# Three projection columns instead of two computed while the input arrives, in a two-layer attention encoder

## The chip, the cores and the metric

The kernel runs on one core of a Trainium2 chip. The metric is the device time of one execution in microseconds; the kernel before has a median of 868.41 us over 3 runs (867.76 to 868.47). Engine names are those of the profile: PE (TensorE, matrix products), PEld (its weight loads), ACT (ScalarE), DVE (VectorE), POOL (GpSimd), SP (SyncE, which here issues nearly all loads).

## The reference

Two layers over 528 tokens (16 meta tokens and a grid of 8 x 64) with 1024 features:

```python
def hybrid_layer(x, norm_g, w_in, q_norm_g, k_norm_g, rpb, w_o_attn, w_o_na, w_out, cos, sin):
    h = rms_norm(x, norm_g)
    proj = jnp.einsum('bld,de->ble', h, w_in)
    qa, ka, va, za, qb, kb, vb, zb, ga, gb = split_cols(proj)
    qa = apply_axial_rope(rms_norm(qa.reshape(b, l, ATTN_HEADS, HEAD_DIM), q_norm_g), cos, sin)
    ka = apply_axial_rope(rms_norm(ka.reshape(b, l, ATTN_KV_HEADS, HEAD_DIM), k_norm_g), cos, sin)
    oa = gqa_attention(qa, ka, va) * jax.nn.silu(za)
    ob = neighbourhood_attention(qb, kb, vb, rpb) * jax.nn.silu(zb)
    mixed = jax.nn.sigmoid(ga) * (oa @ w_o_attn) + jax.nn.sigmoid(gb) * (ob @ w_o_na)
    return x + mixed @ w_out
```

`gqa_attention` is global attention (8 query heads, 2 key heads, head size 64); `neighbourhood_attention` lets each grid token see a window of the grid and the meta tokens. A last `rms_norm` follows the second layer and the meta tokens are dropped.

## The kernel before, in words

Activations lie transposed: a feature tile is 128 features (partitions) by 528 tokens, and there are 8 feature tiles. Weights come in columns of 128 outputs; `w[l, c]` is column `c` of layer `l`, 128 x 1024. Columns 0 to 3 are the global queries (QA), 4 is KA, 5 is VA; then come QB, KB, VB, ZB, ZA (four each), the gates GA and GB, and the output weights. 

Every operand is split into a high part, rounded to fp32r, and a low part, the rest. A product is then three fp32r products: high x high, low x high and high x low. ACT makes the high part by a copy, POOL (weights) or DVE (activations) the low part by a subtraction. One column for all tokens is 8 feature tiles x 3 products x 2 halves of 264 tokens = 48 products, and each half has a PSUM bank of its own.

The normalisation's factor is not applied to the input of the projection: `normed` (L320) multiplies x by the gain only, into `hh` (ACT, L323) and `hl` (DVE, L324). The sum of squares over the features is made beside it: `squared` on ACT (L330), additions on DVE (L401). `norm_split` splits the sum (`ssh`, `ssl`), `norm_root` turns it into 1/rms (`ms` on PE, `mx` on DVE, a power on POOL), and `norm_spread` lays it out as `rbc`, by which VA and the later columns are multiplied when they are read out of PSUM. The queries and KA are normalised per head instead: `rotated` reads a column out on ACT three times (times the gain, L459; the square, rounded, L460, and not, L461), DVE makes `ql`, PE sums the squares per head (`mh`, L444), and `rotate` applies the rotary tables in four DVE operations (L468 to L471).

At the start `piece` loads the first four row tiles of QA and QA+1 in pairs, 128 KB at a time, `half` their second halves, and `feature` one feature tile of x. The products of QA and QA+1 (L423) run as the tiles arrive; QA+2 and all later columns come through `product` (L309 to L311), for which `weights` loads half columns in the order of the list `order`, three ahead, through buffers `raw` (3), `whi` (4) and `wlo` (4).

A scheduler orders each engine's instructions by their place in the program, by readiness in its own time model and by an urgency mark (`high_priority`); `issue_after` puts an instruction behind a named one on its engine. Side work (norm, heads, attention units) is queued by hand: `product` calls `tick()` after each half of a column, and `side_gqa.later(n, part)` puts a part n ticks later. Attention units start at ticks of a given remainder modulo 4: global units at remainder 0, neighbourhood heads at remainder 1. Columns in the dictionary `first` are read out directly and make no tick. `NORM_AT`, `GQA_AT` and `NA_AT` hold the numbers of ticks. Near the end of layer 0 `side_gqa.finish()` (at the third GA gate) runs what is left; one gate column later the product `y` needs the last head's output.

Of the kernel before, what the change touches and what calls it, by code (L numbers as in the profile page):

```python
# [39 lines left out]
NORM_AT = ({"tokens": (1, 4, 6), "squares": (2, 2, 2, 3, 2), "heads": (2, 3, 5, 7, 6), "values": (1, 4)},  # L40
# [51 lines left out]
def trunk_kernel(ctx: ExitStack, tc: tile.TileContext, xT, w, gn, gf, bias, rope, out):  # L92
# [37 lines left out]
    with tc.high_priority():  # L130
        for _ in range(10):
            nc.tensor.matmul(warm[:, :P], zero, zero, start=True, stop=True)


    gains = cpool.tile([P, DEPTH * KT + KT + 2 * DEPTH], F32, name="gains")
# [61 lines left out]
    for l in range(DEPTH):  # L197
        cols = [QA, QA + 1, QA + 2, QA + 3, KA, VA]
        for j in range(4):
            cols += [KB + j, QB + j, VB + j, ZB + j, ZA + j]  # L200
        order += [(l, c, i) for c in cols for i in range(2)]
        if l == 0:

            order = order[1:2] + order[3:]
        for gate, wo in ((GB, WOB), (GA, WOA)):
            for m in range(8 + LAG):
                order += [(l, gate + m, 0), (l, gate + m, 1)] if m < 8 else []
                order += [(l, wo + (m - LAG) // 2, (m - LAG) % 2)] if m >= LAG else []
        order += [(l, WOUT + m, i) for m in range(8) for i in range(2)] if l < DEPTH - 1 else []
# [110 lines left out]
    def normed(l, k, x, n):  # L320

        hi, lo = slot("h", f"hh{l}_{k}", F32R), slot("h", f"hl{l}_{k}", F32R)
        h_last["hi"] = nc.scalar.mul(hi[:, :n], x, g_in[l][:, k:k + 1])  # L323
        h_last["lo"] = nc.vector.scalar_tensor_tensor(lo[:, :n], x, g_in[l][:, k:k + 1], hi[:, :n].bitcast(F32),  # L324
                                                      op0=ALU.mult, op1=ALU.subtract)
        return hi, lo
# [46 lines left out]
    def piece(c, i):  # L373
        raw = slot("K", f"rawp{c}_{i}")[:, :2 * P]
        hi, lo = (slot("O", f"w{'hl'[v]}p{c}_{i}", F32R)[:, :2 * P] for v in range(2))
        nc.sync.dma_start(raw, w[0, c][:, 2 * P * i:2 * P * (i + 1)])
        done[0] = nc.scalar.copy(hi, raw).ins
        done[1] = nc.gpsimd.tensor_sub(lo, raw, hi.bitcast(F32)).ins
        pieces[c, i] = hi, lo

    def half(c):
        weights(0, c, 1, 1)
        done[:] = split_at["weights"]
# [12 lines left out]
    def input_squares(ks):  # L396
        return [squared(k == 0, xs[k], NTOK, f"0_{k}") for k in ks]

    def sum_up(sqs):
        for sq in sqs:  # L400
            nc.vector.tensor_add(total["ss"], total["ss"], sq)  # L401

    total, late = {}, []
    with tc.issue_after(h_last["hi"].ins), tc.issue_after(h_last["lo"].ins):
        total["ss"], *sqs = input_squares(range(3))
        sum_up(sqs)
    with tc.issue_after(h_last["square"].ins):
        weights(0, QA + 2, 1, 1)
    with tc.issue_after(split_at["weights"][0]):
        sum_up(input_squares((3, 4)))  # L410
        late.append(input_squares((5, 6)))


    first, ends = {}, ((0, HALF), (HALF, NTOK))
    for c, ps in ((QA, [bank(ps_p, f"pp0_{QA}_{a}", "pp")[:, :HALF] for a, _ in ends]),
                  (QA + 1, ps_s.tile([P, 2, 512], F32, tag="S", name=f"pp0_{QA + 1}"))):
        first[c] = [(ps[i] if c == QA else ps[:, i, :HALF], a, b) for i, (a, b) in enumerate(ends)]
    for c, k in sorted(((c, k) for c in first for k in range(KT)), key=lambda x: (x[1] + 2 * (x[0] > QA and x[1] > 3), x[0])):
        wh, wl = (t[:, P * (k % 4):P * (k % 4 + 1)] for t in weights(0, c, k // 4, 1)) if k > 3 else (
            t[:, P * (k % 2):P * (k % 2 + 1)] for t in pieces[c, k // 2])  # L420
        for wt, rt in ((wh, 0), (wh, 1), (wl, 0)):
            for ps, a, b in first[c]:
                nc.tensor.matmul(ps, wt, h[k][rt][:, a:b], start=k == 0 and wt is wh and rt == 0,  # L423
                                 stop=k == KT - 1 and wt is wl)

    for l in range(DEPTH):
# [22 lines left out]
        def rotated(c, g, full, name):  # L449
# [8 lines left out]
            for ps, a, b in project(c, full):  # L458
                nc.scalar.mul(q[:, a:b], ps, g)  # L459
                nc.scalar.activation(qh[:, a:b], ps, AF.Square)  # L460
                evac["last"] = nc.scalar.activation(sq[:, a:b], ps, AF.Square)  # L461
# [99 lines left out]
        for j in range(4):  # L561
# [3 lines left out]
            with tc.issue_after(evac["low"].ins):  # L565
                if l == 0 and j < 2:
                    sum_up(late[j])
                if l == 0 and j == 0:
                    turn = rotate
                    with tc.issue_after(evac["last"].ins):  # L570
                        late.append(input_squares((7,)))
# [616 lines left out]
```

## Time and profile before

| | |
|---|---|
| median of 3 runs | 868.41 us (867.76 to 868.47) |
| profiled execution, its own time | 869.61 us |
| its span, first to last instruction | 867.8 us |
| PE busy | 854.8 us (99%), 5976 products |
| ACT, DVE, POOL busy | 494.2, 537.2, 365.6 us |
| HBM read | 76.72 MB |

The profiled execution is one run with a span from the first to the last instruction; its own time lies 1.2 us above the median. PE is the engine that is busy throughout; the end of a product is modelled, so neighbouring products overlap in the busy time, and the starts are the surer measure.

### The profile page before, as it was taken

How to read it: one execution, taken by the hardware profiler on the slowest of the kernel's cores; microseconds unless marked ns; L12 is line 12 of the kernel's file. 1: busy time of each engine (PE TensorE's matmuls, PEld its weight loads, DVE VectorE, ACT ScalarE, POOL GpSimd, SP SyncE). 2: the span in 40 equal slices, each digit the busy share in tenths (PEclk: the TensorE clock that was granted, in tenths of full speed). 3: DMA queues.
4: the chain of work that ended last, by engine and by line, in shares of the span. 5: the costliest groups of instructions: out<-in, count | busy, mean ns of one | idle time of the engine just before them, and what ended most of it. 6: DMA issues, size and time to landing. Idle time of an engine off the chain costs nothing.

```text
span 867.8 us, 16234 instructions
## 1 busy us (share of the span) xinstructions
PE 854.8 (99%) x5976; PEld 790.6 (91%) x5976; DVE 537.2 (62%) x1277; ACT 494.2 (57%) x1170; POOL 365.6 (42%) x300
## 2 busy tenths in 40 slices
PE   8999999999999999999999999999999999999997
PEld 8999999999999999999998989898988888888786
DVE  5985667676774574436547656677767646454633
ACT  7645677677774555333445456677767645543432
POOL 5564323443223332544764643334333333334751
PEclk9999999999999999999999999999999999999999
DMA  6364253325112222325555664235422222223602
GB/s 223 99 186 145 93 150 99 106 73 153 49 50 75 62 67 81 98 86 152 148 139 127 171 198 130 79 95 151 145 81 73 86 73 73 87 85 97 206 25 97
DMA packets 64671, 95.76 MB, mean 110 GB/s; under 512 B 22864, under 2 KB 23376, under 8 KB 64592
## 3 DMA queue, kind: packets, MB, share of 16 engines
q1 hardware_dynamic: 63872, 93.66, 36.8%
q8 instruction: 47, 0.77, 0.4%
q10 hardware_dynamic: 720, 1.06, 0.3%
q14 instruction: 32, 0.26, 0.1%
HBM read 76.72 MB, written 4.19 MB: 93 GB/s over the span
## 4 chain that ended last, share of the span: by engine, by line
PE 86%; ACT 6%; DVE 4%; DMA 2%; issue 1%; POOL 0%; SPq 0%; POOLq 0%; ACTq 0%; DVEq 0%
PE pp L311 18%; PE pp L309 18%; PE pp L310 17%; PE y L309 4%; PE y L311 4%; PE y L310 3%; PE av L797 3%; PE pt L124 3%; PE avb L940 2%; PE pf L1115 2%; PE S L525 2%; PE pf L1117 2%; PE pf L1116 1%; PE S L526 1%; DMA x<-in_xT_dram 1%
## 5 line engine op out<-in xcount | busy, mean ns | idle before, releaser
L227 POOL TENSOR_TENSOR wlo<-raw,whi 128x512 fp32r<-128x512 f32 x214 | 285.3, 1337 | 425.4 <-ACT whi L226 341.7
L309 PE MATMUL pp<-hh,whi 128*128 128x264 f32 (+1 forms) x1056 | 334.7, 317 | 0.6 <-ACT qs L461 0.5
L311 PE MATMUL pp<-hh,wlo 128*128 128x264 f32 (+1 forms) x1056 | 329.3, 312 | 0.0
L310 PE MATMUL pp<-hl,whi 128*128 128x264 f32 (+1 forms) x1056 | 328.6, 311 | 0.0
L226 ACT CAST whi<-raw 128x512 fp32r<-128x512 f32 x214 | 131.5, 619 | 152.7 <-PE pp L310 58.3
L311 PEld LDWEIGHTS pp<-hh,wlo 128*128 128x128 f32 x1056 | 198.8, 188 | 10.7
L309 PEld LDWEIGHTS pp<-hh,whi 128*128 128x128 f32 x1056 | 198.6, 188 | 10.1 <-ACT qs L461 1.1
L310 PEld LDWEIGHTS pp<-hl,whi 128*128 128x128 f32 x1056 | 199.3, 189 | 9.0
L750 DVE CUSTOM_DVE_ANT_1 P<-S,r 128x528 f32<-128x528 f32 x64 | 45.1, 704 | 18.5 <-PE S L526 17.6
L183 DVE TENSOR_TENSOR ptl<-pt,pth 128x512 fp32r<-128x512 f32 x64 | 44.0, 689 | 18.0 <-ACT pth L182 17.2
L1012 DVE TENSOR_TENSOR mg<-pp,rbc 128x264 f32<-128x264 f32 (+1 forms) x48 | 24.8, 517 | 43.2 <-PE pp L311 42.7
L754 ACT ACTIVATE P<-P,st 128x528 f32<-128x528 f32 x64 | 47.2, 737 | 1.9
L876 ACT ACTIVATE Pb<-Pb,stb 128x208 f32<-128x208 f32 (+1 forms) x64 | 31.1, 487 | 16.6 <-DVE stb L874 16.3
L124 PE MATMUL pt<-ident,P 128*128 128x128 f32 x256 | 39.3, 275 | 0.6 <-DVE ptl L183 0.4
L182 ACT CAST pth<-pt 128x512 fp32r<-128x512 f32 x64 | 37.2, 583 | 4.2 <-PE pt L124 2.9
L1013 ACT ACTIVATE mg<-mg 128x264 f32<-128x264 f32 (+1 forms) x48 | 23.7, 494 | 24.4 <-DVE mg L1012 24.4
L310 PE MATMUL pp<-mx,whi 128*128 128x264 f32 x128 | 36.6, 286 | 0.0
L309 PE MATMUL pp<-mx,whi 128*128 128x264 f32 x128 | 36.4, 285 | 0.0
L311 PE MATMUL pp<-mx,wlo 128*128 128x264 f32 x128 | 36.3, 284 | 0.0
L797 PE MATMUL av<-pth,VA 128*128 128x256 f32 x128 | 35.0, 296 | 0.0
L756 DVE TENSOR_SCALAR P<-P,st 128x528 f32<-128x528 f32 x64 | 33.7, 527 | 2.1
L797 PE MATMUL av<-ptl,VA 128*128 128x256 f32 x128 | 33.1, 281 | 0.0
(526 smaller groups left out, 1764.3 us busy)
## 6 DMA issues: line engine op xcount, KB each, us to landing
raw<-in_w_dram SPq DMA_DIRECT2D x214, 256.0 KB, 2.7
bias<-in_bias_dram SPq DMA_DIRECT2D x16, 480.0 KB, 4.5
KB<-KB SPq DMA_DIRECT2D x24, 280.0 KB, 4.0
rawl<-in_w_dram SPq DMA_DIRECT2D x16, 256.0 KB, 2.9
x<-in_xT_dram SPq DMA_DIRECT2D x8, 264.0 KB, 6.3
xr<-in_xT_dram SPq DMA_DIRECT2D x8, 264.0 KB, 3.9
Q<-q SPq DMA_DIRECT2D x16, 128.0 KB, 2.9
x1d<-xt SPq DMA_DIRECT2D x32, 64.0 KB, 2.8
```

The source lines that it names most:

```text
L124: nc.tensor.transpose(ps, src, ident[:n, :n])
L182: split_at["hi"] = nc.scalar.copy(hi, src)
L183: split_at["any"] = nc.vector.tensor_sub(lo, src, hi.bitcast(F32))
L226: cast = nc.scalar.copy(hi, raw)
L227: sub = nc.gpsimd.tensor_sub(lo, raw, hi.bitcast(F32))
L309: nc.tensor.matmul(ps, wh, rh[:, a:b], start=i == 0, stop=False)
L310: nc.tensor.matmul(ps, wh, rl[:, a:b], start=False, stop=False)
L311: nc.tensor.matmul(ps, wl, rh[:, a:b], start=False, stop=i == n - 1)
L750: newest["max"] = nc.vector.tensor_tensor_reduce(p[:n].rearrange("p (i k) -> p i k", i=2), S[:n, :, :HALF], scale[:n].unsqueeze(2).to_broa ...
L754: nc.scalar.activation(p[:n], p[:n], AF.Exp, bias=st[:n, 1:2], scale=1.0, accum_out=st[:n, 2:3])
L756: nc.vector.tensor_scalar_mul(p[:n], p[:n], st[:n, 3:4])
L797: nc.tensor.matmul(c["av"], rows2(c["t"][i][0]), c["t"][i][1], start=i == 0, stop=i == 8)
```

## The change

- QA, QA+1 and QA+2 run with the input. Their weights are laid out on the host by row tiles: `w3[k]` holds the 128 inputs of feature tile k for all 384 outputs, 192 KB in one piece. `row_tile(k)` loads and splits it in front of `feature(k)`; the loads of weights and x are put in turn on SP. `w3[0]` is loaded from ACT's queue, ahead of the gains.
- hh of feature tile 0 is made in two halves of the tokens.
- Squares are computed and added along with the tiles, three tiles behind; tiles 6 and 7 are added after QA and QA+1 are read out. The first half column of QA+3 is cast after the sixth square.
- The products go tile by tile over three columns up to tile 3, and then in a written order. QA+2 gets two PSUM banks of another pool (`avn`, `avg`).
- The read-outs in `rotated` follow each other on ACT. In layer 0 the ticks of `norm_split`, `norm_root`, `norm_spread` are 1, 2, 4 instead of 1, 4, 6, those of the first two sums of squares per head 1, 1 instead of 2, 2, and `meta_columns` 4 instead of 5. QA+2 makes no ticks any more.
- 7 warming products instead of 10 (two records each).

```diff
-NORM_AT = ({"tokens": (1, 4, 6), "squares": (2, 2, 2, 3, 2), "heads": (2, 3, 5, 7, 6), "values": (1, 4)},
+NORM_AT = ({"tokens": (1, 2, 4), "squares": (1, 1, 2, 3, 2), "heads": (2, 3, 5, 7, 6), "values": (1, 4)},
...
-        for _ in range(10):
+        for _ in range(7):
             nc.tensor.matmul(warm[:, :P], zero, zero, start=True, stop=True)
+    w3 = w[0, QA:QA + 3].rearrange("c p n -> (c p n)").rearrange("(k p n) -> k p n", k=KT, p=P)
+    raw3 = {0: slot("K", "rawp0")[:, :3 * P]}
+    nc.scalar.dma_start(raw3[0], w3[0])
...
-            order = order[1:2] + order[3:]
+            order = order[6:]
...
-    def normed(l, k, x, n):
+    def normed(l, k, x, n, spans=None):
         hi, lo = slot("h", f"hh{l}_{k}", F32R), slot("h", f"hl{l}_{k}", F32R)
-        h_last["hi"] = nc.scalar.mul(hi[:, :n], x, g_in[l][:, k:k + 1])
+        for a, b in spans or ((0, n),):
+            h_last["hi"] = nc.scalar.mul(hi[:, a:b], x[:, a:b], g_in[l][:, k:k + 1])
...
-    def piece(c, i):
-        raw = slot("K", f"rawp{c}_{i}")[:, :2 * P]
-        hi, lo = (slot("O", f"w{'hl'[v]}p{c}_{i}", F32R)[:, :2 * P] for v in range(2))
-        nc.sync.dma_start(raw, w[0, c][:, 2 * P * i:2 * P * (i + 1)])
...
+    def row_tile(k):
+        if k not in raw3:
+            raw3[k] = slot("K" if k < 4 else "E", f"rawp{k}")[:, :3 * P]
+            in_turn(raw3[k], w3[k])
+        hi, lo = (slot("O", f"w{'hl'[v]}p{k}", F32R)[:, :3 * P] for v in range(2))
+        done[0] = nc.scalar.copy(hi, raw3[k]).ins
+        done[1] = nc.gpsimd.tensor_sub(lo, raw3[k], hi.bitcast(F32)).ins
+        pieces[k] = hi, lo
     def feature(k):
         if k % 2 == 0:
             xs.extend(two("M", f"x0_{k}"))
-        nc.sync.dma_start(xs[k], xT[k])
-        h.append(normed(0, k, xs[k], NTOK))
+        in_turn(xs[k], xT[k])
+        h.append(normed(0, k, xs[k], NTOK, ((0, HALF), (HALF, NTOK)) if k == 0 else None))
         done[0] = h_last["hi"].ins
-    for part in ((piece, QA, 0), (feature, 0), (piece, QA + 1, 0), (feature, 1), (piece, QA, 1), (piece, QA + 1, 1),
-                 (feature, 2), (feature, 3), (half, QA), (feature, 4), (half, QA + 1), (feature, 5), (feature, 6), (feature, 7)):
-        in_order(lambda: part[0](*part[1:]))
...
+    for k in range(KT):
+        in_order(lambda: row_tile(k))
+        in_order(lambda: feature(k))
+        if k > 2:
+            in_order(lambda: add_up(k - 3))
+    in_order(lambda: add_up(5))
+    in_order(next_weights)
...
+    def first_products(c, k):
+        wh, wl = (t[:, P * (c - QA):P * (c - QA + 1)] for t in pieces[k])
+        for wt, rt in ((wh, 0), (wl, 0), (wh, 1)):
+            for ps, a, b in first[c]:
+                nc.tensor.matmul(ps, wt, h[k][rt][:, a:b], start=k == 0 and wt is wh and rt == 0,
+                                 stop=k == KT - 1 and rt == 1)
+    for k in range(4):
+        for c in range(QA, QA + 3):
+            first_products(c, k)
+    for c, k in ((0, 4), (1, 4), (0, 5), (1, 5), (0, 6), (2, 4), (0, 7), (1, 6), (1, 7), (2, 5), (2, 6), (2, 7)):
+        first_products(QA + c, k)
...
             for ps, a, b in project(c, full):
-                nc.scalar.mul(q[:, a:b], ps, g)
-                nc.scalar.activation(qh[:, a:b], ps, AF.Square)
-                evac["last"] = nc.scalar.activation(sq[:, a:b], ps, AF.Square)
+                with ExitStack() as held:
+                    if "last" in evac:
+                        held.enter_context(tc.issue_after(evac["last"].ins))
+                    nc.scalar.mul(q[:, a:b], ps, g)
+                    nc.scalar.activation(qh[:, a:b], ps, AF.Square)
+                    evac["last"] = nc.scalar.activation(sq[:, a:b], ps, AF.Square)
...
                 if l == 0 and j < 2:
-                    sum_up(late[j])
+                    with tc.issue_after(evac["last"].ins):
+                        add_up(6 + j)
...
-                    side_gqa.later(5, meta_columns)
+                    side_gqa.later(4, meta_columns)
...
+    w[0, QA:QA + 3] = w_in[0][:, :3 * P].reshape(3, P, KT * P)
```

More of the change, by code (lines that the diff above doesn't have):

```diff
@@ L371, in in_order @@
             part()
-    def piece(c, i):
-        raw = slot("K", f"rawp{c}_{i}")[:, :2 * P]
-        hi, lo = (slot("O", f"w{'hl'[v]}p{c}_{i}", F32R)[:, :2 * P] for v in range(2))
-        nc.sync.dma_start(raw, w[0, c][:, 2 * P * i:2 * P * (i + 1)])
[L377 to L383, printed above, removed]
+    def row_tile(k):
[6 more added lines that the diff above has]
+        pieces[k] = hi, lo
     def feature(k):
@@ L396, in input_squares @@
[L396 to L411, printed above, removed]
+    total = {}
@@ new lines, in square, with add_up, next_weights @@
+    def square(k):
+        sq = squared(k == 0, xs[k], NTOK, f"0_{k}")
+        done[0] = h_last["square"].ins
+        return sq
+    def add_up(k):
+        sq = square(k)
+        if k == 0:
+            total["ss"] = sq
+        else:
+            nc.vector.tensor_add(total["ss"], total["ss"], sq)
+    def next_weights():
+        weights(0, QA + 3, 0, 1)
+        done[:] = split_at["weights"]
+    for k in range(KT):
[3 more added lines that the diff above has]
+            in_order(lambda: add_up(k - 3))
@@ L414, in trunk_kernel @@
+    in_order(lambda: add_up(5))
+    in_order(next_weights)
     first, ends = {}, ((0, HALF), (HALF, NTOK))
+    two_banks = ps_s.tile([P, 2, 512], F32, tag="S", name=f"pp0_{QA + 1}")
     for c, ps in ((QA, [bank(ps_p, f"pp0_{QA}_{a}", "pp")[:, :HALF] for a, _ in ends]),
[L416 to L421, printed above, removed]
+                  (QA + 1, [two_banks[:, i, :HALF] for i in range(2)]),
+                  (QA + 2, [bank(ps_a, f"pp0_{QA + 2}_{tag}", tag)[:, :HALF] for tag in ("avn", "avg")])):
+        first[c] = [(ps[i], a, b) for i, (a, b) in enumerate(ends)]
```

3 lines of the change are left out of this document (removed).

## The prediction

> **What bounds the kernel now.** I read the page first, then the granted clock and busy time in chosen stretches, then the start in order of time, engine by engine, and last the waits of PE.
>
> ```profile
> span 867.8 us, 16234 instructions
> PE 854.8 (99%) x5976; PEld 790.6 (91%) x5976; DVE 537.2 (62%) x1277; ACT 494.2 (57%) x1170; POOL 365.6 (42%) x300
> 5.33:26.74 21.41, 19.63 (x146) 18.25 (x146) 15.69 (x22) 18.37 (x39) 10.87 (x9) 1.00 0.57 193
> PE pp L423 <- DVE hl L324: 1.3, 3, 0.7
> PE pp L309 <- ACT qs L461: 0.5, 1, 0.5
> PE S L526 <- DVE KA0l L516: 0.5, 1, 0.5
> ```
>
> PE is busy nearly all the span, and the number of products does not change, so only PE's pauses can be won. Busy time hides short ones, because the modelled ends overlap. I count starts instead, in the timeline of PE:
>
> ```profile
> 1.04 4.64 PE L132 MATMUL warm<-zero 128*128 128x128 f32 x20 [1.04 <-DVE one L138]
> 5.33 0.76 PE L423 MATMUL pp<-hh,whp 128*128 128x264 f32 x2
> 5.91 0.42 PE L423 MATMUL pp<-hl,whp 128*128 128x264 f32 x2
> 16.04 0.40 PE L423 MATMUL pp<-hl,whi 128*128 128x264 f32 x2
> 19.94 0.40 PE L423 MATMUL pp<-hh,wlo 128*128 128x264 f32 x2
> 20.79 0.39 PE L309 MATMUL pp<-hh,whi 128*128 128x264 f32 x1 [0.46 <-ACT qs L461]
> 26.74 0.28 PE L444 MATMUL mh<-qh,means_r 128*10 128x264 f32 x1
> ```
>
> From 16.04 to 19.94, 32 products start without a break: 3.90 / 32 = 0.122 us each. A unit, one weight column of one feature tile, is 6 products, 0.731 us. The first three q columns are 24 units, 17.55 us, and end where the row `mh` starts, at 26.74, having begun at 5.33. So 21.41 - 17.55 = 3.9 us of that stretch are pauses. That, and a little before 5.33, is all the change can win at the start.
>
> The pauses come from ACT and DVE, which make the operands as the input lands:
>
> ```profile
> 4.07 0.73 ACT L323 ACTIVATE hh<-x,gains 128x528 fp32r<-128x528 f32 x1 [0.75 <-DMA x<-in_xT_dram]
> 7.05 0.70 ACT L377 CAST whp<-rawp 128x256 fp32r<-128x256 f32 x2
> 10.18 0.74 ACT L323 ACTIVATE hh<-x,gains 128x528 fp32r<-128x528 f32 x1 [1.26 <-DMA x<-in_xT_dram]
> 12.89 2.16 ACT L323 ACTIVATE hh<-x,gains 128x528 fp32r<-128x528 f32 x3
> 16.56 1.13 ACT L226 CAST whi<-raw 128x512 fp32r<-128x512 f32 x2
> 17.59 2.24 ACT L330 ACTIVATE sq<-x 128x528 f32<-128x528 f32 x4
> 6.40 6.47 DMA x<-in_xT_dram
> ```
>
> The last row is of the chain of waits: x7 lands at 12.87. Two columns are 1.46 us of PE work for each feature tile, while the first four tiles come (10.18 - 4.07) / 3 = 2.0 us apart.
>
> **The change part by part.**
>
> *Three columns per feature tile (gain, 3.1 us).* With three units (2.19 us) a tile, PE should fall behind the input and stop waiting. The first product starts when the first half of hh0 is done: x0 moves to the front of SP's queue, but 192 KB of weights travel beside it instead of 128 KB, so I leave hh0 at 4.1; half of it takes about 0.4. PE then does four products, waiting for wlp0 and hl0, until about 5.5, and the first unit ends near 5.95. The other 23 units take 16.8, to 22.8.
>
> From the fourth feature tile on the suppliers are as tight as PE. ACT does per tile a cast of 384 columns (between 0.35 each in the row with 256 and 0.56 in the one with 512: 0.46), hh (2.16 / 3 = 0.72) and a square (2.24 / 4 = 0.56): 1.74 us. DVE does hl and an addition of squares, and these depend on what POOL does beside them:
>
> ```profile
> 4.84 0.77 DVE L324 SCALAR_TENSOR_TENSOR hl<-x,gains,hh 128x528 fp32r<-128x528 f32 x1 [2.54 <-ACT hh L323]
> 16.43 1.50 DVE L401 TENSOR_TENSOR sq<-sq,sq 128x528 f32<-128x528 f32 x2
> 18.26 3.10 DVE L401 TENSOR_TENSOR sq<-sq,sq 128x528 f32<-128x528 f32 x2 [0.32 <-ACT sq L330]
> 7.51 1.74 POOL L378 TENSOR_TENSOR wlp<-rawp,whp 128x256 fp32r<-128x256 f32 x2 [1.30 <-ACT whp L377]
> 17.24 3.56 POOL L227 TENSOR_TENSOR wlo<-raw,whi 128x512 fp32r<-128x512 f32 x2 [2.66 <-ACT whi L226]
> ```
>
> An addition takes 0.75 before POOL's 17.24 and 1.55 beside it. POOL will subtract for eight row tiles of 384 columns, some 1.1 us each (0.87 for 256, 1.78 for 512), so about 60% of DVE's time has POOL beside it: 0.9 + 1.2 = 2.1 us a tile against PE's 2.19. With 1.55 for every addition, hl5, hl6 and hl7 come late by some 1.7 in all and the three columns end at 24.5; with 0.75 for each, at 22.8. I take 23.6, nearer the 60%. 26.74 - 23.6 = 3.1 us (2.2 to 3.9).
>
> [...]
>
> *The loads.* In front of x7 go 8 x 192 = 1536 KB of weights instead of 1024 KB. The window before it moved about 395 KB/us at the end:
>
> ```profile
> GB/s 0 0 0 0 0 95 236 266 214 338 370 278 308 289 222 273 111 175 309 287 292 284 348 366 308 255 301 354 384 408 409 368 416 410 389 407 405 409 396 393
> ```
>
> 512 / 395 = 1.3 us, so x7 lands at 14.2, while PE reaches (0,7) after some 18.5. Four microseconds cover it; without them it would be 1.3 us. On SP the loads stand in turn, w1 behind x0; w0 leaves ACT's queue ahead of `gains`, which may hold hh0 by a few tenths (inside the 0.8 between the bounds). Casts of row tiles 4 to 7 need the O buffers of tiles 0 to 3, which PE releases from 7.4 on, before ACT gets there.
>
> *Fewer warming products (nothing, to 1.5 us lost).* 14 instead of 20 records, 4.64 / 20 = 0.23 each, end at about 4.2 instead of 5.5. PE was slow until about 5.9: the pair at 5.33 took 0.76, the next one 0.42. The gap until the first real product is a tenth or two, so I take nothing.
>
> *The weights of the fourth column (loss, 0.5 us).* Only the first half of QA+3 is cast ahead. The second is wanted 12 products after 23.6, at 25.1. In the old order ACT cast the later weights only between evacuations:
>
> ```profile
> 19.74 0.46 ACT L459 ACTIVATE q<-pp,gains 128x264 f32<-128x264 f32 x1
> 24.39 1.65 ACT L226 CAST whi<-raw 128x512 fp32r<-128x512 f32 x3
> 25.08 4.48 POOL L227 TENSOR_TENSOR wlo<-raw,whi 128x512 fp32r<-128x512 f32 x3 [4.28 <-ACT whi L226]
> ```
>
> If it stays there, at 24.4, POOL's part (4.48 / 3 = 1.5) is done at 26.6 and PE waits 1.5; if ACT takes it in the pause before QA is finished, nothing. Evacuations of the three columns in a row are the worst case, 2 us. I take 0.5. The bank wait of 0.5 in the row of waits lies inside the stretch counted above and goes with it: QA is read out while the other columns run.
>
> *The order written for the sums (loss, 0.5 us).* A column in `first` makes no tick, so QA+2 no longer makes two. `norm_split` stays one tick after QA, but that tick is now in QA+3, and `norm_root` follows one tick later, not three. What it waits for:
>
> ```profile
> 27.59 0.64 ACT L182 CAST ssh<-sq 128x528 fp32r<-128x528 f32 x1
> 30.05 1.79 DVE L469 TENSOR_TENSOR qr<-qr,sin 128x528 f32<-128x528 f32 x1
> 31.76 0.69 DVE L183 TENSOR_TENSOR ssl<-sq,ssh 128x528 fp32r<-128x528 f32 x1
> 33.57 0.16 PE L356 MATMUL ms<-means_r,ssh 128*128 128x2 f32 x1
> ```
>
> Now ssl ends 1.1 before PE asks. After, PE asks at 23.6 + 0.5 + 2 x 2.93 + 1.0 (eight mh products) = 31.0; ssh again follows the mh products, which free its buffers, at about 27.8, and ssl two DVE operations of up to 1.8 later: 29.8 to 32.4. PE waits nothing to 1.4; half a microsecond is taken. Behind ms stands all of KA.
>
> *Attention later by two ticks (gain, 0.5 us).* The first global unit starts at the tick divisible by four that it had, 12, now after VB0 and not after QB0. The wait for KA0l (0.5 in the row) is covered by a product more. At the layer's end the last unit finishes inside the cover of one gate:
>
> ```profile
> 347.94 0.28 PE L797 MATMUL av<-pth,VA 128*128 128x256 f32 x1
> 351.32 0.71 DVE L183 TENSOR_TENSOR oa_3b<-oa,oa_3a 128x528 fp32r<-128x528 f32 x1 [0.70 <-ACT oa_3a L182]
> 354.39 0.28 PE L309 MATMUL y<-oa_0a,whi 128*128 128x264 f32 x1
> ```
>
> oa_3 is ready 2.4 us before y starts. After, transposes and their split (about 1.3 for ACT and DVE), meta and sums fall behind that gate too, some 2.4 more, so the cover is just used up: 0 to 1.5, taken at 0.2.
>
> Sum: 3.1 - 0.5 - 0.5 + 0.5 - 0.2 = 2.4 us. The profiled execution would go from 867.8 to 865.4 in span, and from 869.61 to 867.2 in its own time, which is 1.2 above the median shown; the median goes from 868.41 to 866.0.
>
> **The rivals.** *DVE sets the pace further on.* It runs without pause until 57:
>
> ```profile
> 21.70:57.00 35.30, 35.20 (x290) 33.97 (x289) 34.48 (x62) 19.98 (x48) 20.52 (x17) 1.00 0.50 141
> 45.11 0.28 PE L444 MATMUL mh<-ql,means_r 128*10 128x264 f32 x1
> 48.26 0.42 DVE L664 TENSOR_TENSOR va<-pp,rbc 128x264 f32<-128x264 f32 x1
> 48.74 0.39 PE L309 MATMUL pp<-hh,whi 128*128 128x264 f32 x1
> ```
>
> The first half of VA was finished before 44.8 and was read at 48.26; its bank was taken again at 48.74. If DVE keeps its order and moves only by the one addition it has already done, 0.7, PE waits for that bank and the time is 867.7. Against it: the evacuation is marked urgent, so an earlier PE puts it ahead of rotations, which the later first unit lets wait.
>
> *The root comes too early (slower).* If the third column's split and rotation (0.7 + 0.8 + 1.8 + 1.8 + 0.7 = 5.8 beside POOL) stand in front of ssl on DVE, it ends at about 37, PE stands 6 us before ms, and the time is 868.4 - 2.9 + 6 = 871.5. It decides from the point where ssl ends later than 31.0 + 2.9 = 33.9; over 0.2% it needs 35.6. For it: the split now lies one column later in program order. Against: it is marked urgent, and in the rows above it came between the products of a rotation.
>
> *The clock opens later.* The granted clock of the quoted stretch is 1.00, but PE was slow from 1.04 to 5.9, 4.9 us. If the pause after the shorter warming made that time start over at 4.2, half rate would last to 9.1, and 3.2 us of it cost 1.6: 867.6. Against it: the pause is short beside 4.9. [...]
>
> **How the numbers follow.** A measurement of this kernel tells 0.2%, 1.7 us, from no change. The forecast, a gain of 1.8 or more, holds 0.55 (its own range 864.3 to 866.6); DVE's pace 0.22 and the clock 0.08, both within 0.2%; the early root 0.15, of which 0.12 over 0.2% slower. So faster 0.55, same 0.33, slower 0.12. The range goes from 864.3, all terms at their good ends, to 869.6, which takes in the rivals of no change and some of the early root.
>
> **What would show it.** Three columns ending on PE before 24.5, with waits of PE for hl under 1.7 us in all; x7 landed before 15; a cast of QA+3's second half before 24.5; no wait of PE at ms; S of the first unit without a wait, after VB0; from 60 us on PE's rows as before but 2 to 3 us earlier. It is wrong if PE waits at ms, at `pp` for `va`, or at y in the layer's tail by more than 1.5, or if a slow pitch lasts beyond 7 us.

## The result: 0.5% slower, and where the time went

| | before | after |
|---|---|---|
| median of 6 runs each, one chip | 868.53 us (867.76 to 869.32) | 873.57 us (871.28 to 874.54) |
| ratio, 95% interval | | 1.0052 [1.0038, 1.0066] |
| profiled execution, own time; span | 869.61; 867.8 us | 873.49; 871.7 us |

The prediction said 866.0 us (864.3 to 869.6). The profiled execution after lies at its median; the one before lies 1.1 us above its own. I therefore profiled the kernel before a second time (e11: own time 868.77, span 867.0) and compare with that. Its gain on the first lies at the start, as its first three columns end at 25.60 and not at 26.74, and 0.8 us of it is still there at layer 1. The page of after begins:

```profile
span 871.7 us, 16225 instructions
PE 855.4 (98%) x5970; PEld 792.1 (91%) x5970; DVE 532.9 (61%) x1277; ACT 493.7 (57%) x1171; POOL 366.9 (42%) x300
```

The work is the same, so the starts tell more. I cut each execution at three products: the first one, the first one after the three columns, the first `rk` (the factors of KA, before the first attention unit), and the first `mh` of layer 1. Rows are stretch, length, busy time by engine (PE, PEld, DVE, ACT, POOL), granted clock, DMA share and GB/s. The second profile of before, then after:

```profile
5.32:25.60 20.28, 19.08 (x147) 18.22 (x147) 14.92 (x22) 18.32 (x39) 10.55 (x9) 1.00 0.58 202
25.60:57.46 31.86, 31.80 (x263) 30.58 (x260) 29.79 (x54) 16.46 (x37) 20.49 (x17) 1.00 0.53 149
57.46:458.69 401.23, 398.78 (x3225) 389.87 (x3223) 245.25 (x625) 229.56 (x565) 163.37 (x130) 1.00 0.36 103
```

```profile
5.89:25.27 19.38, 19.38 (x145) 19.24 (x146) 16.12 (x15) 16.32 (x35) 14.73 (x13) 0.91 0.66 223
25.27:60.23 34.96, 33.56 (x262) 32.06 (x261) 27.96 (x60) 18.64 (x44) 18.24 (x15) 0.95 0.45 121
60.23:463.50 403.27, 398.99 (x3224) 390.18 (x3223) 242.72 (x625) 229.10 (x564) 163.58 (x130) 1.00 0.36 102
```

The three columns end at 25.27 instead of 25.60: 0.3 us won, where 3.1 was forecast. The way to `rk` then takes 34.96 instead of 31.86 us, 3.1 lost. The 400 us from there to layer 1, where the diff touches nothing, take 403.27 instead of 401.23, 2.0 lost; the remainder is the same within 0.1. The sum, 4.7, is the difference of the two executions' times (873.49 - 868.77).

*At the start* PE waits for its first operand, then runs at half rate:

```profile
1.04 3.29 PE L132 MATMUL warm<-zero 128*128 128x128 f32 x14 [1.04 <-DVE one L142]
5.89 0.51 PE L432 MATMUL pp<-hh,whp 128*128 128x264 f32 x2 [1.56 <-ACT hh L328]
9.11 0.64 PE L432 MATMUL pp<-hh,whp 128*128 128x264 f32 x2
12.14 0.40 PE L432 MATMUL pp<-hh,whp 128*128 128x264 f32 x2
```

ACT, which makes that operand, and the loads from ACT's queue (count, size, us from issue to landing):

```profile
4.64 0.51 ACT L383 CAST whp<-rawp 128x384 fp32r<-128x384 f32 x1 [1.50 <-DMA rawp<-in_w_dram]
5.32 0.92 ACT L328 ACTIVATE hh<-x,gains 128x264 fp32r<-128x264 f32 x2 [0.17 <-DMA gains<-in_gains_dram]
```

```profile
rawp<-in_w_dram ACTq DMA_DIRECT2D x1, 192.0 KB, 3.9
gains<-in_gains_dram ACTq DMA_DIRECT2D x1, 14.0 KB, 4.1
```

The first weights are there at 4.6 and the gains at 5.3, and `hh` of tile 0, which the prediction put at 4.1, begins at 5.32. The products at 9.11 take 0.64 a pair, those at 12.14 0.40. The two stretches in which the clock was half:

```profile
7.54:10.96 3.42, 3.42 (x18) 3.42 (x17) 3.42 (x3) 3.42 (x8) 3.42 (x4) 0.50 1.04 360
38.26:41.68 3.42, 3.42 (x18) 3.42 (x17) 3.42 (x7) 1.11 (x4) 2.11 (x4) 0.50 0.54 144
```

By these rows, 3.42 us at a granted clock of 0.50 cost 1.7. One of them lies in each of the first two stretches; neither is in the second profile of before. (Before the first opening the granted clock stands at 1.00 even where products are slow, in e1's profile from 4.2 to 10.2, and the mean clock of a run leaves it out: 0.999 in the profile of e7, which opened at 9.6. So a late opening is read from the pace of the products: a pair of 128x264 takes 0.64 at half rate and 0.40 at full.)

*Behind the three columns* PE stands at `ms`. Rows of the list of PE's waits over the whole execution (total, times, longest):

```profile
PE vtd L693 <- DVE na L747: 2.0, 6, 0.7
...
PE Sm L543 <- DVE st L767: 1.5, 1, 1.5
...
PE ms L361 <- DVE ssl L187: 0.8, 1, 0.8
PE mh L459 <- DVE ql L481: 0.6, 1, 0.6
PE pt L124 <- DVE VB L187: 0.6, 1, 0.6
...
PE pp L313 <- DVE mg L1029: 0.4, 1, 0.4
```

The wait for KA0l, 0.5 before, is gone, as the prediction said. In its place `vtd` has 2.0 instead of 1.3, and Sm (1.5), VB (0.6) and mg (0.4) are new, all in the attention. Between 58 and 463 us, where the second profile of before has these two as its longest,

```profile
PE pt L124 <- DVE P L756: 0.6, 1, 0.6
PE S L526 <- DVE KA0l L516: 0.5, 1, 0.5
```

all waits of PE add up to 2.2 us there and to 4.2 in after: the difference is the 2.0 lost. The largest, on PE and then on DVE and POOL at that place:

```profile
264.44 0.34 PE L543 MATMUL Sm<-KA0h,Q2m 128*64 128x264 f32 x1 [1.50 <-DVE st L767]
...
261.84 1.80 DVE L736 TENSOR_TENSOR ob<-ob,zb 128x528 f32<-128x528 f32 x1
263.67 0.71 DVE L767 CUSTOM_DVE_ANT_1 P<-S,r 128x528 f32<-128x528 f32 x1
261.79 2.98 POOL L231 TENSOR_TENSOR wlo<-raw,whi 128x512 fp32r<-128x512 f32 x2 [1.67 <-ACT whi L230]
```

The scores S of a global unit are ready when DVE has just begun the last product of a neighbourhood head (`ob` by its gate). That product takes 1.80 us beside POOL's subtraction, the softmax's maximum waits for it, and the next scores, Sm, wait for the softmax to free their bank.

### The profile page after: what moved, and what is told of

Same layout as the page of the kernel before. It is cut to its first block, busy times and chain, and to the rows that moved or that the text cites. A ratio compares the mean times of both kernels' runs of the same rounds, so it can differ in the third digit from the quotient of the medians.

```text
span 871.7 us, 16225 instructions
## 1 busy us (share of the span) xinstructions
PE 855.4 (98%) x5970; PEld 792.1 (91%) x5970; DVE 532.9 (61%) x1277; ACT 493.7 (57%) x1171; POOL 366.9 (42%) x300
## 3 DMA queue, kind: packets, MB, share of 16 engines
q1 hardware_dynamic: 63728, 93.46, 37.1%
## 4 chain that ended last, share of the span: by engine, by line
PE 88%; ACT 5%; DVE 4%; issue 1%; DMA 1%; POOL 0%; POOLq 0%; ACTq 0%
PE pp L315 18%; PE pp L313 18%; PE pp L314 18%; PE y L313 4%; PE y L315 4%; PE y L314 3%; PE av L814 3%; PE pt L124 3%; PE avb L957 2%; PE pf L1132 2%; PE S L543 2%; PE pf L1134 2%; PE pf L1133 1%; PE S L544 1%; PE pp L432 1%
## 5 line engine op out<-in xcount | busy, mean ns | idle before, releaser
L231 POOL TENSOR_TENSOR wlo<-raw,whi 128x512 fp32r<-128x512 f32 x210 | 279.8, 1336 | 425.7 <-ACT whi L230 326.5
L313 PE MATMUL pp<-hh,whi 128*128 128x264 f32 (+1 forms) x1040 | 330.2, 318 | 0.4 <-DVE mg L1029 0.4
L315 PE MATMUL pp<-hh,wlo 128*128 128x264 f32 (+1 forms) x1040 | 325.7, 313 | 0.0
L314 PE MATMUL pp<-hl,whi 128*128 128x264 f32 (+1 forms) x1040 | 324.7, 312 | 0.0
L230 ACT CAST whi<-raw 128x512 fp32r<-128x512 f32 x210 | 129.0, 619 | 156.0 <-PE pp L314 61.0
L315 PEld LDWEIGHTS pp<-hh,wlo 128*128 128x128 f32 x1040 | 196.4, 189 | 10.7
L313 PEld LDWEIGHTS pp<-hh,whi 128*128 128x128 f32 x1040 | 196.3, 189 | 9.7 <-DVE mg L1029 0.6
L314 PEld LDWEIGHTS pp<-hl,whi 128*128 128x128 f32 x1040 | 196.9, 189 | 8.9
L771 ACT ACTIVATE P<-P,st 128x528 f32<-128x528 f32 x64 | 47.2, 738 | 1.9
L814 PE MATMUL av<-pth,VA 128*128 128x256 f32 x128 | 35.2, 296 | 0.0
```

The lines of the kernel that those rows point to most:

```text
L230: cast = nc.scalar.copy(hi, raw)
L231: sub = nc.gpsimd.tensor_sub(lo, raw, hi.bitcast(F32))
L313: nc.tensor.matmul(ps, wh, rh[:, a:b], start=i == 0, stop=False)
L314: nc.tensor.matmul(ps, wh, rl[:, a:b], start=False, stop=False)
L315: nc.tensor.matmul(ps, wl, rh[:, a:b], start=False, stop=i == n - 1)
L771: nc.scalar.activation(p[:n], p[:n], AF.Exp, bias=st[:n, 1:2], scale=1.0, accum_out=st[:n, 2:3])
```

## The experiments

The main theory is that of the phase: the shift of the attention by one product puts neighbourhood heads and global units into each other's way. Its rivals: the loss is at the start, by late operands or by the clock; the order written for the sums (`ms` too early) costs it; and, from the prediction, DVE's pace takes back what the start wins. Where an expectation names a theory by a letter, C is the phase. Ratios are to the kernel before, run on the same chip.

**Three warming products more (e1).**

```diff
-        for _ in range(7):
+        for _ in range(10):
```

> The changed kernel with 10 warming products again (20 records, to about 5.3 us). Theory A, the granted clock: the pause of PE from 4.2 to 5.9 us is what put the clock to half from 7.5 to 11.0; without the pause the clock stays open there, the three columns end near 23.6 instead of 25.3, and the execution is 1 to 1.7 us shorter than the changed kernel's 873.5, near 872. The second slow window, after the pause at ms, stays. Rival B, the input alone: the start at 5.9 is set by the landing of the first weights, the warming only fills the pause; then the columns end at 25.3 as before and the time is that of the changed kernel within 0.5.

Measured: 872.65 us (870.93 to 873.89), 1.0040 [1.0026, 1.0053], against after's 1.0052: the intervals overlap. In its profile the clock opened only at 10.2, although PE had been warming to 5.68, and it closed again later:

```profile
37.52:40.94 3.42, 3.42 (x17) 3.42 (x17) 3.42 (x6) 0.58 (x2) 3.19 (x5) 0.50 0.44 110
```

Ten products did not open the clock earlier here (10.2) than seven in after (4.1), and the three stretches together lose as much as in after. The number of warming products is not the main cause.

**The first weights by SP's queue (e2).**

```diff
-    nc.scalar.dma_start(raw3[0], w3[0])
+    nc.sync.dma_start(raw3[0], w3[0])
```

> The changed kernel with the first row tile of weights issued by SP, ahead of x0, and only the gains from ACT's queue. Theory A: the late start comes from the first weights and the gains sharing the DMA engines with later tiles from the other queue; on SP in turn they land by 3.3 and 3.1, hh0 starts by 4.4, PE's first product by 4.9, the pause behind the warming is under 0.8 us, the clock stays open, and the three columns end near 23. Gain over the changed kernel 1.5 to 2.5 us, to 871 to 872. Rival: first tiles land late because eight transfers share the engines whichever queue issues them; hh0 starts at 5.0 or later and the time moves by under 0.5.

Measured: 871.50 us (870.53 to 872.65), 1.0036 [1.0023, 1.0048]. ACT has its operands 1.3 to 1.5 us earlier:

```profile
3.18 0.51 ACT L383 CAST whp<-rawp 128x384 fp32r<-128x384 f32 x1 [0.52 <-DMA rawp<-in_w_dram]
4.07 0.92 ACT L328 ACTIVATE hh<-x,gains 128x264 fp32r<-128x264 f32 x2 [0.38 <-DMA x<-in_xT_dram]
```

The first product starts at 4.64 instead of 5.89. The three stretches:

```profile
4.64:24.28 19.64, 18.69 (x144) 17.92 (x145) 16.35 (x15) 16.48 (x35) 14.10 (x13) 1.00 0.70 248
24.28:57.76 33.48, 32.10 (x263) 30.60 (x262) 30.78 (x61) 18.75 (x44) 18.18 (x15) 1.00 0.47 125
57.76:461.25 403.49, 399.03 (x3224) 390.21 (x3223) 243.27 (x625) 228.99 (x564) 164.27 (x130) 1.00 0.36 102
```

The granted clock is 1.00 from start to `rk` here, so these rows show the change without a half-rate stretch: the columns end 1.3 earlier than before (24.28 against 25.60), `rk` comes 0.3 later than before, and the attention still loses 2.3 (403.49 against 401.23). The late start is not enough to explain the loss.

**The root later (e3).** The third sum of squares per head comes one tick later too.

```diff
-NORM_AT = ({"tokens": (1, 2, 4), "squares": (1, 1, 2, 3, 2), ...
+NORM_AT = ({"tokens": (1, 3, 4), "squares": (1, 1, 3, 3, 2), ...
```

> The changed kernel with norm_root one tick later (tokens 1, 3, 4) and the third sum of squares per head one tick later (squares 1, 1, 3). Theory A: PE's waits for ql (0.9) and ssl (1.0) at 32 to 36 us go, and with them the slow window from 38.3 to 41.7; VA begins 1.5 to 3 us earlier and the execution gains as much, to 870.5 to 872. Rival: DVE is the pace there, and PE waits the same time at the read-out of VA or at KB0; then VA's or KB0's products start no earlier, and the time stays within 0.5 of 873.5.

Measured: 871.95 us (870.66 to 872.07), 1.0038 [1.0026, 1.0051]. The wait at `ms` is gone, and so is the second half-rate stretch; a wait of 0.5 at `rb` for POOL's root takes its place. `rk` comes at 58.7 instead of 60.2, about the 1.7 that such a stretch costs. All five runs have a mean granted clock of 0.998; the two runs of after whose clock closed least (0.999) took 871.6 on average, no more. So what e3 wins by its median looks like the clock's, and the attention still takes 403.2 us (58.68 to 461.90).

**The two ticks of QA+2 given back (e4).**

```diff
                     evac["last"] = nc.scalar.activation(sq[:, a:b], ps, AF.Square)
+                if l == 0 and c == QA + 2:
+                    tick()
...
-NORM_AT = ({"tokens": (1, 2, 4), "squares": (1, 1, 2, 3, 2), ...
+NORM_AT = ({"tokens": (1, 4, 6), "squares": (2, 2, 2, 3, 2), ...
...
-                    side_gqa.later(4, meta_columns)
+                    side_gqa.later(5, meta_columns)
```

> The changed kernel with two ticks made at the read-out of QA+2, one for each half, and the numbers of ticks of the kernel before, so that norm, heads and attention units stand beside the same products as before. Theory C: the shift by two ticks is what costs PE 2.3 us between 60 and 400 us (waits at Sm 1.7, at vtd and mg 1.2, at pt 0.7) and the waits at ms and mh 1.9 with the clock's second window 1.7; with the ticks back, the second layer starts within 0.5 of the kernel before, and the time is 868 to 870. Rival: DVE is behind from the start, so the waits move to KA0l at the first global unit (more than 2 us) and the time stays above 871.

Measured: 871.90 us (871.72 to 872.44), 1.0042 [1.0029, 1.0054], not the 868 to 870 expected. Two effects of opposite sign. The old tick numbers put `rb` ahead of its root, one wait:

```profile
PE rb L567 <- POOL rx L197: 3.0, 1, 3.0
```

That and another half-rate stretch (37.1 to 40.5; the run's mean clock is 0.996, e3's 0.998) bring `rk` to 61.63. But from there to layer 1 it takes 400.17 us:

```profile
61.63:461.80 400.17, 398.70 (x3225) 389.98 (x3224) 244.80 (x625) 229.63 (x564) 163.16 (x130) 1.00 0.37 103
```

So the ticks act on the attention as the theory of the phase says; the start and the order for the sums are not mended by them.

**Only the attention's phases (e5).** Without touching the start, the remainders at which units begin move by two ticks:

```diff
-GQA_AT_TICK, NA_AT_TICK = (0, 0), (1, 1)
+GQA_AT_TICK, NA_AT_TICK = (2, 2), (3, 3)
```

> The changed kernel with the remainders at which attention units start moved by two (global units 2 for 0, neighbourhood heads 3 for 1, both layers), so that the units stand beside the products as in the kernel before, while the norm stays as changed. Theory C, the units' place: from the products rk of layer 0 to the first mh of layer 1 the changed kernel lost 2.4 us against the kernel before (offsets 1.6 and 4.0); with the units back it loses nothing there or wins up to 0.7, and the time falls by 2 to 3, to 870 to 871.5; the long gap of 1.8 before Sm is gone. Rival: that loss comes from the time that the start lost, as units and read-outs collide in any place; then the offset still grows by more than 1.5 us.

Measured: 869.03 us (867.46 to 870.46), 1.0009 [1.0000, 1.0018]. Against after the median is 4.5 us lower; by the ratios, which allow for the chip, 3.7. The second and third stretch, and DVE at the place of the long wait:

```profile
25.11:60.07 34.96, 33.55 (x263) 32.06 (x262) 28.01 (x60) 18.63 (x44) 18.23 (x16) 0.95 0.44 120
60.07:460.41 400.34, 398.79 (x3224) 390.05 (x3223) 244.82 (x625) 229.65 (x564) 162.99 (x130) 1.00 0.36 103
```

```profile
258.90 0.71 DVE L736 TENSOR_TENSOR ob<-ob,zb 128x528 f32<-128x528 f32 x1
```

Everything up to `rk` is as in after, 34.96 us, with its `ms` pause and half rate. The attention takes 400.34 instead of 403.27, 2.9 less; the waits at Sm, VB and mg are absent, and the gate's product takes 0.71, with POOL idle beside it. All waits of PE between 58 and 463 us add up to 1.3 instead of 4.2, which is the same 2.9. The rest of the difference goes with how often the clock closed in the runs: those of e5 with a mean clock of 0.998 or 0.999 average 868.5, those of after with 0.999 871.6, again 3 apart. e5 moves the remainders in layer 1 too, where no tick had been taken away; from its first `mh` to the end the kernel takes 408.3 us, as before (408.3) and after (408.2). The phase is shown as the larger part of the loss.

**The converse: the kernel before, with the ticks shifted (e8).** QA+2 makes no ticks, and `NORM_AT` and `meta_columns` get after's numbers:

```diff
-NORM_AT = ({"tokens": (1, 4, 6), "squares": (2, 2, 2, 3, 2), ...
+NORM_AT = ({"tokens": (1, 2, 4), "squares": (1, 1, 2, 3, 2), ...
...
-            tick()
+            if (l, c) != (0, QA + 2):
+                tick()
```

> The kernel before, with two columns at the start, but QA+2 makes no ticks and the norm has the changed numbers of ticks (1, 2, 4; 1, 1, 2). Theory C: the shift of the attention units and of the norm alone costs what the changed kernel shows, 2 to 4 us without any change of the start; from rk to layer 1 it loses 2 to 2.5. Rival: the shift is harmless with the old start; the time stays within 0.7 of 868.5.

Measured: 876.51 us (876.42 to 876.82), 1.0095 [1.0081, 1.0108]. With the old start the attention loses the same:

```profile
63.42:466.55 403.13, 398.82 (x3224) 389.98 (x3223) 242.93 (x625) 228.94 (x564) 163.91 (x130) 1.00 0.36 102
```

Its longest waits of PE:

```profile
PE ms L357 <- DVE ssl L183: 2.3, 1, 2.3
...
PE Sm L526 <- DVE st L751: 1.5, 1, 1.5
```

The wait at Sm is there again with the same 1.5. The shorter delay of the root costs 2.3 at `ms` here and two half-rate stretches in a row (35.1 to 41.9), so that `rk` comes at 63.4; that part depends on the start, and it makes the whole loss 8.4 us, more than the 2 to 4 expected.

**Fewer warming products in the kernel before (e7).**

```diff
-        for _ in range(10):
+        for _ in range(7):
```

> The kernel before with 7 warming products instead of 10, nothing else. The pause of PE lasts from 4.2 to about 5.0 us (hh0 is ready at 4.8). Theory A, the granted clock: in the executions in which a slow window falls on 7 to 11 us the start loses up to 1.7 us; over several executions the median is 0.3 to 1.5 us longer and the times scatter more. Rival: a pause of under 1 us does not matter to the clock, and the start may even come earlier by 0.3; the time stays within 0.3 of the kernel before.

Measured: 868.44 us (867.81 to 870.04), 1.0005 [0.9997, 1.0014]. In its profile the clock opened at 9.6 and the three columns ended at 25.9, 0.3 later than in the second profile of before. The warming is worth 0.05%, not told from nothing.

**All mends together (e6).** The edits of e1, e2, e3 and e5 in the kernel after:

```diff
+        for _ in range(10):
+    nc.sync.dma_start(raw3[0], w3[0])
+NORM_AT = ({"tokens": (1, 3, 4), "squares": (1, 1, 3, 3, 2), ...
+GQA_AT_TICK, NA_AT_TICK = (2, 2), (3, 3)
```

> The changed kernel with four repairs: first weights by SP, 10 warming products, the root one tick later (tokens 1, 3, 4, squares 1, 1, 3), and the units' remainders moved by two. If the costs found so far stand side by side, the three columns end near 24.3 (as with the first weights by SP), the waits at ms and the second slow window are gone, and the middle of layer 0 loses nothing: 866.5 to 868.5. If DVE sets the pace between 25 and 60 us, the early end of the three columns is lost again at rb, at the read-out of VA or at KA0l, and the time is 868.5 to 870.

Measured: 868.01 us (867.32 to 869.47), 0.9999 [0.9990, 1.0008]: its median is 5.6 us below after's, and it is no better than before. The medians of the four alone lie 0.9 + 2.1 + 1.6 + 4.5 = 9.1 below after's, so the gains don't add up; in part the mends take away the same half-rate stretches. The three stretches:

```profile
5.32:23.71 18.39, 17.93 (x146) 17.73 (x146) 16.41 (x15) 16.12 (x34) 13.62 (x10) 1.00 0.72 252
23.71:56.86 33.15, 32.00 (x263) 30.52 (x262) 30.79 (x61) 18.71 (x44) 19.05 (x15) 1.00 0.44 126
56.86:457.33 400.47, 398.66 (x3224) 390.04 (x3223) 245.30 (x625) 229.53 (x564) 163.55 (x130) 1.00 0.36 103
```

Now the three columns end at 23.7, the 23.6 of the prediction, 1.9 earlier than before. Of that 1.3 is given back by `rk`. (This execution is the quickest of the eleven of e6, 0.7 below their median, and the second profile of before lies 0.3 above its own; so about 1 us by which e6 is ahead in these rows is the choice of executions.) DVE is the engine to look at. From the first product to `rk` it is busy 14.92 + 29.79 = 44.7 us before and 16.41 + 30.79 = 47.2 here, for the same 74 instructions: the eight `hl` take 10.0 us instead of 6.8 and the seven additions of squares 7.7 instead of 6.3, and the other work takes 2 less. In the second stretch DVE is busy 93% of the time in both. ACT is busy as long as before (34.8).

**Eight warming products for ten, in e6 (e9).**

```diff
-        for _ in range(10):
+        for _ in range(8):
```

> The four repairs of e6 with 8 warming products instead of 10, so that the warming ends at 4.4 and does not hold the first product (hh0 is ready at 4.5). If the start is still what counts, the three columns end 0.5 to 0.7 earlier than in e6 and the time is 867.3 to 867.7. If DVE sets the pace up to 60 us, the time stays at 868.0 within 0.3, whatever the start wins.

Measured: 868.17 us (867.41 to 868.85), 0.9996 [0.9988, 1.0005]. The first product comes 0.7 earlier (4.64), the columns end at 23.75 and `rk` comes at 56.9, as in e6. An earlier first product alone gives nothing. That the suppliers then set the end of the columns is an inference: PE's only wait there is again 0.5 for `hl`.

**Stacked pairs one column later (e10).** This kernel has e9's eight warming products, though its expectation calls it e6.

```diff
-            if j > 1:
-                stack_pair(j - 2)
+            if j > 1 + (l == 0):
+                stack_pair(j - 2 - (l == 0))
...
+        if l == 0:
+            stack_pair(1)
```

> e6 with the stacking of the query pairs one column later in layer 0, so that ACT's copy of Q no longer stands, waiting 1.9 us for the rotation, in front of the read-out of QA+3 and of ssh. Theory D, the order on ACT: KA's first bank comes free and ssh is made about 2 us earlier, PE's waits at mh (0.9) and rb (0.8) go, and the time falls by 1 to 1.7, to 866.3 to 867. Rival, DVE or its buffers: the read-out waits for a buffer that a rotation frees, the gaps stay or move to KA0l at the first global unit (now 0.8), and the time stays within 0.4 of 868.

Measured: 867.93 us (867.07 to 869.12), 0.9994 [0.9985, 1.0003]; e9, from which it is one edit away, has 868.17. The wait at `rb` is gone, and a longer one at the third sum of squares stands in its place. The row of PE's waits, and the timeline with DVE's rotation ahead of `ql`, a later one, POOL, and the two halves of the sum of squares:

```profile
PE mh L459 <- DVE ql L481: 1.8, 1, 1.8
```

```profile
30.43 1.79 DVE L487 TENSOR_TENSOR qr<-qr,sin 128x528 f32<-128x528 f32 x1
32.14 0.69 DVE L481 TENSOR_TENSOR ql<-qs,qh 128x528 fp32r<-128x528 f32 x1
35.71 0.70 DVE L487 TENSOR_TENSOR qr<-qr,sin 128x528 f32<-128x528 f32 x1
30.22 1.43 POOL L231 TENSOR_TENSOR wlo<-raw,whi 128x512 fp32r<-128x512 f32 x1 [2.16 <-ACT whi L230]
30.60 0.63 ACT L186 CAST ssh<-sq 128x528 fp32r<-128x528 f32 x1
35.09 0.69 DVE L187 TENSOR_TENSOR ssl<-sq,ssh 128x528 fp32r<-128x528 f32 x1
```

`ql` waits in DVE's queue behind a product that takes 1.79 beside POOL's subtraction and 0.70 at 35.71, without it. ACT now makes `ssh` at 30.60, 2.7 earlier than in after, as the theory of ACT's order wanted. Yet DVE reaches `ssl` at 35.09, as in after (35.18): rotations and `ql` stand in front of it.

**That sum behind KA's first half (e12).** DVE's order stays to the letter; PE's four `mh` of QA+2 move.

```diff
+                last_mm[0] = nc.tensor.matmul(ps, wl, rh[:, a:b], start=False, stop=i == n - 1)
...
+                    with ExitStack() as held:
+                        if l == 0 and j == 2:
+                            held.enter_context(tc.issue_after(last_mm[0].ins))
...
```

> The kernel with all mends and the two stacked pairs spaced out, and of it only the third sum of squares (four products mh) put behind the first half of KA on PE. DVE keeps its order to the letter. Before, PE stood 2.03 us at this sum, from 30.9 to 32.9, waiting for ql, and then found ssl ready at ms (36.2). Theory that DVE sets the pace here: ssl still ends at 35.8, PE now reaches ms at 34.0 and stands 1.5 to 2 there; rk is earlier by 0 to 0.4 than the 57.4 before, the time stays at 867.9 (867.4 to 868.4), ratio to the kernel before 0.999 to 1.000. Rival, that PE's own order costs the 2 us: ms waits less than 0.5, rk comes at 55.4, and the time goes to 866.0 (865.5 to 866.8), the first version that is faster than the kernel before.

Measured: 868.66 us (867.57 to 870.50), 1.0005 [0.9996, 1.0014]. The wait moves to the next thing that DVE owes:

```profile
PE ms L361 <- DVE ssl L187: 1.9, 1, 1.9
```

```profile
35.40 0.70 DVE L187 TENSOR_TENSOR ssl<-sq,ssh 128x528 fp32r<-128x528 f32 x1
```

So DVE's pace is shown up to `ssl`: giving PE other work doesn't help, DVE hands over `ssl` at the same place, 35.40 where e10 had 35.09. In the profile the clock then closed from 37.9 to 41.4 (a product of 128x264 takes 0.42 there and 0.28 ahead of it), which the wait in e10 had not brought about, and `rk` came at 59.25 and not by the 57.4 expected; the two runs with a mean clock of 0.999 took 867.6, the seven with 0.996 or 0.997 took 869.1 on average, and two with 0.994 870.3. The rival's 866.0 is not reached in any of them.

## Why the prediction was wrong, step by step

**Attention later by two ticks: forecast a gain of 0.5, measured a loss of 2.0.** The three steps that failed missed by similar amounts in the profiles, 2.5 us here, 2.8 and 2.6 in the two below. This one has the clearest proof: mended alone (e5) it takes the time to 869.03, and none of the other mends alone goes below 871.5. I priced the shift by the wait for KA0l and the layer's tail. Neither cost anything (no wait for KA0l, and oa_3 ready 1.7 before y, where I had taken a loss of 0.2). What I left out is that units are laid against products by ticks: with two ticks fewer, every head and unit of layer 0 runs beside other products, and other DVE and POOL work, than before. The price stands in one stretch: from `rk` to layer 1 it is 403.1 to 403.5 us in the five kernels measured with shifted ticks (after, e1, e2, e3, e8) and 400.2 to 401.2 in eight profiles with the old phase (before twice, e4, e5, e6, e9, e10, e12); e7, also with the old phase, has 402.0, with waits of 0.9 each for KA0l and P. Of the difference, 1.5 is the softmax behind the gate's product. That e5 is 0.9 quicker than the second profile of before lies in the 0.5 for KA0l and in 0.4 less at P (0.2 for 0.6). Why VB and `vtd` come late in the shifted kernels was not followed up.

**Three columns per feature tile: forecast 3.1, measured 0.3; 1.3 with the clock open (e2).** Three parts. First, my reference was one execution whose columns ended at 26.74; the second profile has 25.60, so 1.1 of the gain was the chance of one profile. Second, `hh` of tile 0 at 4.1: I let the weights ahead of `gains` cost a few tenths, inside the bounds, and they cost 1.2, as both took about 4 us from issue to landing. With SP's queue `hh` starts at 4.07 and the columns end at 24.28; with the other mends at 23.7. Third, the half-rate stretch, below. The sizing of the suppliers, 22.8 to 24.5, held once these were out of the way. One sum is off too: with all terms at their good ends the gain is 3.9 + 0.5 = 4.4, so the low end of the range would be 864.0 and not 864.3.

**Fewer warming products: forecast nothing.** The gap that I called "a tenth or two" was 1.56, and a slow pace beyond 7 us, which I had named as a sign of being wrong, came. The price is near that of the rival "the clock opens later", 1.7 against 1.6, but the form is another: the clock opened near 4.1 (the last warming record takes 0.35, those ahead of it 0.42) and closed again from 7.54 to 10.96. Over the runs the number of warming products is worth little, though: 0.05% in e7, and e1, with ten, opened at 10.2. The two half-rate rows of after last 3.42 us each, and the clock opened at 4.1 in after's profile, at 9.6 in e7's and at 10.2 in e1's, where PE had been issuing since 1.04, 9.2 us before, with a pause of 0.35 ahead of the product at 6.02. What sets these times is not shown.

**The order for the sums: forecast a loss of 0.5, 0 to 1.4; the wait is 0.8, and more hangs on it.** ssl ended at 35.9, not between 29.8 and 32.4: three columns side by side finish QA later, so ACT reads it out from 21.7 instead of 19.7, and ssh came at 33.3, behind a copy of Q that stood 1.9 us for DVE's rotation:

```profile
31.71 0.62 ACT L499 CAST Q<-q 128x512 fp32r<-128x512 f32 x1 [1.90 <-DVE q L489]
```

e10 took that wait away and ssl came no earlier, so DVE's own order holds it back as well. The wait stayed at 0.8 because PE was late too: it stood at `ms` from 35.2, not from 31.0. What the term lacked besides is the clock. Half-rate stretches between the columns' end and `rk` appear only in profiles where the list of waits has 0.7 or more at `ms` or `rb` (after, e1, e4, e5, e8, e12) and in none where it has 0.5 or less (before, e3, e6, e7, e9, e10); e2 paused at `ms` too and kept its clock in the profile. So a pause there goes with the closing, and the price is then about 1.7 more. That the pause is its cause is an inference from these profiles: e10 paused 1.8 at `mh` and kept its clock, and no run changed the pause alone. The stretch from the columns' end to `rk` is 3.1 longer in after than before, so 1.7 of it is this half rate and the waits at `ms` and `mh` are 1.4.

**The loads and the weights of the fourth column: right.** ACT has no wait for input after the first tiles, and casts the fourth column's weights from 18.66. The 0.5 that I set aside was not needed.

**The rivals.** "DVE sets the pace" at 867.7 is what the mended kernels do (867.9 to 868.7), though by another wait than the bank of `va`: `ql`, `ssl` and the root; shown is DVE's pace up to `ssl`, not beyond. "The root comes too early" came true in its half about ssl: I wrote that it decides from ssl at 33.9 and shows from 35.6, and it was 35.9. Its other half, PE standing 6 us at `ms`, did not, since PE came there 4 us later than I assumed; that its 871.5 is near the runs of after with an open clock is chance, as most of that is the attention.

None of the mended versions e6, e9, e10 and e12 is told from the kernel before: their ratios lie between 0.9994 and 1.0005, with intervals within 0.9985 to 1.0014.

## What to carry to other kernels

When an edit removes ticks, slots or turns from a hand-laid schedule, price the phase of all that is scheduled by them, not only the first unit: compare one late stretch, in which nothing was edited, before anything else. When PE is freed at the start, look at the busy share of the next engine in the following stretch; at the 93% of DVE here there was little to win by moving PE's work. And take a second profile of the kernel before, if a term of the sum is as large as the scatter of its runs.

## What the runs showed of the hardware

In six profiles of these kernels (after, e1, e4, e5, e8, e12) the granted clock closed between the columns' end and `rk`, in or behind a pause of PE of 0.7 to 3.0 us at `ms` or `rb`. It stood at 0.50 for 3.42 us in after (from 38.26) and in e1 (from 37.52), about as long in e4 (from 37.1) and in e12 (from 37.9), and for 6.83, twice that, in e8 (from 35.08); in e5 its mean from 25.11 to 60.07 was 0.95, as in after's second stretch. One with such a pause of 0.7 (e2) kept its clock, and that the pause is the cause is not shown. The clock first opened anywhere from 4.1 to 10.2 us: with seven warming products at 4.1 in after and at 9.6 in e7, with ten at 10.2 in e1. Of after's runs, the two with a mean clock of 0.999 took 871.6 us on average, the two with 0.997 873.7, the one with 0.996 874.5 and the one with 0.994 873.5.

On DVE the product with the rotary table (128 x 528) takes 0.70 us with POOL idle (at 35.71) and 1.79 beside a subtraction of POOL (from 30.43, POOL's from 30.22 to 31.65), in the rows of e10; `ql` behind it starts at 32.14, and PE waited 1.8 for that. Why the product is longer there is not shown.
